# A hybrid attention and SSM layer on one core: SSM before the q/k projection's leftovers, GLU ahead of attention, cache work last, SSM products in pairs

## The chip, the cores and the metric

The kernel runs on one core of a Trainium2 chip. The metric is the device time of one execution in microseconds (us), lower is better. Of the kernel before there are three timed runs, and beside them one profiled execution, from which all rows below come.

## What is computed

One layer, for a prompt of 2048 tokens and a sample of 64 tokens whose past of 1024 keys and values comes from a cache. `proj = x @ w_in` gives q, k, v (512 columns each) and u (512 columns). Half of the width is differential attention (8 heads, two softmax maps each, block-causal), the other half an S5 state space model (SSM) in 32 groups of 16 channels with a 64-dimensional complex state each:

```python
bu = einsum('blgc,gpc->blgp', u, bb)              # input to the states
h  = associative_scan(complex h = lb*h + bu)      # prompt from 0, sample from h0
y  = Re(einsum('blgp,gcp->blgc', h, c)) + d*u     # out of the states
z  = gelu(y) @ w_glu + b_glu ; ssm_out = z[:512] * sigmoid(z[512:])
mix = concat(attention, ssm_out) @ w_out
x1 = LN(alpha*x + mix) ; x2 = LN(alpha*x1 + relu(x1 @ w_up)^2 @ w_down)
```

Outputs are x2, the rotated keys, the values and the last SSM states.

## The kernel before, in words

Large products are done in three passes of float32r pieces (`mm3`, L136 to L139: high by high, low by high, high by low), so an operand is first split into a high part (L131 or L133) and a low part (L134). The SSM's own products are float32 and appear twice per product among the matmul records.

Stages, in the order of the code: `proj_uv` makes u (PSUM tile `pu`) and v (`pv`) for all tokens; `proj_qk` makes q and k (PSUM tile `pm`, transposes `pt`) in 17 tiles of 128 tokens and stores them transposed to DRAM (`s_q`, `s_k`); `attention_all` runs the heads in four sets of query tiles (scores `sps`, transposed weights `tps`, values `oT`); `glu` turns the stored SSM result into the second half of the mix (PSUM `za`, `zb`); `blocks` runs w_out (`pd`), the norm and the feed-forward part (`pu`, `pd`) for four blocks of 512 tokens.

The SSM runs in four batches of eight groups. `ssm_build` makes a batch's matrices: `em` (input), `gf` (powers of the transition), `km` (the direct part, made from the products `psk` and a trip through DRAM, `s_kp`) and `et` (rotations, on POOL). `ssm_run` loads u as `ug`, makes `psi` = em by ug, rotates (`turn`), scans along time (L883), rotates back into `vt`, and then for each group makes `psy` = km by ug plus two products gf by vt (real and imaginary part, 64 rows each: group 2q uses rows 0 to 63, group 2q+1 rows 64 to 127). GELU is made from two ACT and two DVE instructions on `gy`, which is stored to `s_gy`. The GLU loads all of it back (`gyg`, four loads of 1060 KB) with its weights (`wrg`).

`cache_keys` copies the cached values (`cvr` to `s_vc`) and splits the cached keys (`ckr`, `ckh`, `ckl` to `s_kc`). Its result is first read by the sample units of the third attention set.

What sets the order: a scheduler sorts each engine's instructions at build time by readiness and priority. Code under `level(n)` has priority n*100000 above the rest, attention runs at HIP = 200000. While `proj_qk` runs, each of its steps is followed by ten steps of the SSM generator `fl` (priority U8); from step CK0 = 6 on, also by one step of `cache_keys`. The GLU runs as filler of the attention stage at priority U4. Each engine then takes its list strictly in order; all loads and stores go through SP's list, so one that waits holds all behind it.

Of the kernel before, what the change touches and what calls it, by code (L numbers as in the profile page):

```python
# [29 lines left out]
HD = 64  # L30
NMAP = 16
G = 32
PS = 64
C = 16
T = 8
JP = SEQ // T
NJ = JP + 1 + DEC // T
# [29 lines left out]
CK0 = 6  # L67
# [4 lines left out]
U8 = 0  # L72
# [8 lines left out]
U1, U2, U4 = 2, 3, 0  # L81
# [33 lines left out]
def build(nc, tc, io, ctx):  # L115
# [25 lines left out]
    def tt(e, out, a, b, op):  # L141
        e.tensor_tensor(out=out, in0=a, in1=b, op=op)  # L142
# [125 lines left out]
    def split_v(vv, v):  # L268
        split(vv[:, :, 0], vv[:, :, 1], v.rearrange("p (h d) -> p h d", d=HD), hi_eng=dve, lo_eng=pool)
# [125 lines left out]
    def cache_keys(c2):  # L395
        op = c2.enter_context(tc.tile_pool(name="ck", bufs=CKB, side="right"))
        for i in range(PAST // 128):
            raw = op.tile([128, 512], F32, tag="ckr", name="cvr")
            dma(out=raw, in_=io["cv"][i * 128:i * 128 + 128, :])
            for q, t_ in enumerate("hl"):  # L400
                vv = op.tile([128, 4, 2, HD], F32R, tag="ck" + t_, name="cvv")
                split_v(vv, raw[:, q * 256:q * 256 + 256])
                dma(out=VC.rearrange("h p i e d -> p i h (e d)")[:, i, q * 4:q * 4 + 4], in_=vv.rearrange("p h e d -> p h (e d)"))
            if i % 2:
                yield
        for c in range(4):
            for hf in range(2):
                h = op.tile([128, 512], F32R, tag="ckh", name="ckh")
                l = op.tile([128, 512], F32R, tag="ckl", name="ckl")
                rr, cc = slice(c * 128, (c + 1) * 128), slice(hf * 512, hf * 512 + 512)  # L410
                raw = op.tile([128, 512], F32, tag="ckr", name="ckr")
# [5 lines left out]
                yield  # L417
# [264 lines left out]
    def ssm_disc(kp, sp):  # L682
# [62 lines left out]
        ss.dsb = kp.tile([C, G], F32, name="dsb")  # L745
# [11 lines left out]
    def ssm_build(w, bt):  # L757

        ss = k.ss
# [8 lines left out]
        m.gf = w.kp.tile([128, 2, HP, 9, C], F32, tag="gf", name="gf", bufs=MB)  # L770
        m.et = w.kp.tile([128, 2, HP, NJ], F32, tag="et", name="et", bufs=EB)
# [36 lines left out]
        k0 = bp.tile([128, HG, 128], F32, tag="btm", name="k0")[0:C]  # L808
        dd = bp.tile([C, HG, C], F32, tag="dd", name="dd")
        for e in range(2):  # L810
            psk = pm.tile([C, HP, 128], F32, tag="pi", name="psk", bufs=IB)
            o = slice(e * 64, e * 64 + 64)
            for q in range(HP):
                for ri in range(2):
                    pe.matmul(psk[:, q, :], lhsT=bb[o, ri, q, :], rhs=m.gf[o, ri, q, 0:8, :].rearrange("p t c -> p (t c)"),
                              start=ri == 0, stop=ri == 1)
            act.activation(out=k0.rearrange("c (q e) n -> c e q n", e=2)[:, e], in_=psk, func=AF.Copy)
        tt(dve, dd, ss.dsb[:, gs].unsqueeze(2).to_broadcast([C, HG, C]), ident[0:C, 0:C].unsqueeze(1).to_broadcast([C, HG, C]), ALU.mult)
        tt(dve, k0[:, :, 0:C], k0[:, :, 0:C], dd, ALU.add)
        dma(out=KP[:, gs, 112:240], in_=k0)  # L820
# [15 lines left out]
        pool.tensor_copy(out=e[:, :, :, JP:NJ], in_=e[:, :, :, 0:NJ - JP])  # L836
        w.mats = m
        yield

    def ssm_run(w, m, bt):  # L840
# [10 lines left out]
        z = bp.tile([128, 2, HP, NJ], F32, tag="z", name="z", bufs=ZB)  # L851
# [28 lines left out]
        for ri in range(2):  # L880
            for q in range(HP):
                for c0, c1, i in ((0, JP, 0.0), (JP + 1, NJ, h0[:, ri, q:q + 1])):
                    dve.tensor_tensor_scan(out=z[:, ri, q, c0:c1], data0=ss.rho[:, bt * HP + q:bt * HP + q + 1].to_broadcast([128, c1 - c0]),  # L883
                                           data1=v[:, ri, q, c0:c1], initial=i, op0=ALU.mult, op1=ALU.add)
# [4 lines left out]
        for g in range(HG):  # L889
            psy = pm.tile([128, 512], F32, tag="ps", name="psy")  # L890
            y = psy[:, :NJ]
            o = slice(g % 2 * 64, g % 2 * 64 + 64)
            pe.matmul(y, lhsT=m.km[:, g, :], rhs=ug[:, g, :], start=True, stop=False)
# [3 lines left out]
            gy = sp.tile([128, NJ], F32, tag="gy", name="gy", bufs=GB)  # L897
            act.activation(out=gy, in_=y, func=AF.Square, scale=math.sqrt(0.044715))
            dve.scalar_tensor_tensor(out=gy, in0=gy, scalar=1.0, in1=y, op0=ALU.add, op1=ALU.mult)
            act.activation(out=gy, in_=gy, func=AF.Tanh, scale=GC)  # L900
            dve.scalar_tensor_tensor(out=gy, in0=gy, scalar=1.0, in1=y, op0=ALU.add, op1=ALU.mult)
            gg = bt * HG + g
            dma(out=GY[gg * C:(gg + 1) * C, :, :].rearrange("c t j -> t c j"), in_=gy)
            if g % 4 == 3:
                yield
# [326 lines left out]
    with ExitStack() as c1:  # L1232
# [253 lines left out]
```

## Time and profile before

| | us |
|---|---|
| median of three runs | 3104.84 (3096.53 to 3106.6) |
| profiled execution | 3110.11 |
| its span | 3108.3 |
| PE busy | 2884.2 (93%) |
| DVE, ACT, POOL busy | 1755.3, 1504.1, 1649.0 |

The span has these stages: u and v up to about 205 us, q/k with the SSM up to about 525 us, attention set 0 with the GLU up to about 757 us, then w_out and the feed-forward part beside the other attention sets up to about 2030 us, and the feed-forward part of the last blocks alone to the end. A matmul's end is modelled, so the place of a product is best read from where the next one starts.

### The profile page before, as it was taken

The page shows a single profiled execution, that of the slowest core. Times are in us where ns is not written, and L with a number is a line of the kernel's source. Part 1 is how long each engine was busy: PE and PEld are TensorE (multiplying, and loading weights), DVE is VectorE, ACT ScalarE, POOL GpSimd, SP SyncE. Part 2 cuts the span into 40 slices and gives each one's busy share as a digit, 9 for nine tenths or more (in the row PEclk, how much of TensorE's full clock was granted, in tenths as well). Part 3 has the DMA queues.
Part 4 walks back from the last instruction along what each step waited for, and adds up shares of the span by engine and source line. Part 5 has one row for each costly group of instructions (what it writes and reads, how often), then busy time and mean ns, then how long its engine had stood idle before and what let it go on. Part 6 is the DMA issues. An engine that isn't in the chain of part 4 may idle for free.

```text
span 3108.3 us, 46420 instructions
## 1 busy us (share of the span) xinstructions
PE 2884.2 (93%) x15648; PEld 2418.0 (78%) x15648; DVE 1755.3 (56%) x4631; ACT 1504.1 (48%) x2905; POOL 1649.0 (53%) x1552
## 2 busy tenths in 40 slices
PE   8999999799889999999869999988799999989996
PEld 7976666698778888887659888866688888868885
DVE  7126876588687655657787666545526222442224
ACT  4222233687676766665568767532323333323332
POOL 2227762355665566655646656544545444555554
PEclk9999999699989999999879999999899999999998
DMA  6368784656744444445634333266322222253332
GB/s 189 121 200 222 203 231 140 209 160 200 210 133 135 129 127 124 120 128 185 182 107 126 109 106 95 80 196 193 92 84 69 79 82 81 83 169 95 99 99 71
DMA packets 419619, 424.42 MB, mean 137 GB/s; under 512 B 53394, under 2 KB 312978, under 8 KB 418356
## 3 DMA queue, kind: packets, MB, share of 16 engines
q1 hardware_dynamic: 419380, 421.46, 46.6%
q8 instruction: 123, 2.02, 0.3%
q14 instruction: 116, 0.95, 0.1%
HBM read 327.71 MB, written 93.64 MB: 136 GB/s over the span
## 4 chain that ended last, share of the span: by engine, by line
PE 58%; DVE 13%; DMA 10%; issue 4%; ACT 3%; POOL 3%; SPq 1%; DVEq 0%; POOLq 0%; ACTq 0%
PE pd L137 7%; PE pd L138 7%; PE pd L139 7%; PE pu L137 7%; PE pu L139 6%; PE pu L138 6%; PE oT L579 3%; PE tps L563 3%; PE sps L516 2%; DVE acc L142 2%; DMA raw<-in_w_up 2%; DMA raw<-in_ln_g 2%; DVE s L519 2%; ACT s L527 1%; DMA raw<-in_w_out 1%
## 5 line engine op out<-in xcount | busy, mean ns | idle before, releaser
L134 POOL TENSOR_TENSOR dl<-raw,dh 128x512 fp32r<-128x512 f32 x336 | 437.1, 1313 | 312.5 <-ACT dh L131 269.6
L134 POOL TENSOR_TENSOR fwl<-raw,fwh 128x512 fp32r<-128x512 f32 x256 | 332.3, 1301 | 351.6 <-ACT fwh L131 314.1
L519 DVE TENSOR_SCALAR_CACHE_REDUCE s<-sps 128x512 f32<-128x512 f32 (+5 forms) x688 | 401.4, 599 | 192.6 <-PE sps L516 115.6
L137 PE MATMUL pu<-bxh,fwh 128*128 128x256 f32 (+2 forms) x1472 | 490.4, 335 | 14.3 <-ACT fr L1178 8.6
L142 POOL TENSOR_TENSOR s<-s 128x512 f32<-128x512 f32 (+3 forms) x344 | 383.2, 1138 | 206.8 <-ACT s L547 182.8
L138 PE MATMUL pu<-bxl,fwh 128*128 128x256 f32 (+2 forms) x1472 | 487.0, 332 | 0.0
L139 PE MATMUL pu<-bxh,fwl 128*128 128x256 f32 (+2 forms) x1472 | 483.7, 333 | 1.9 <-POOL fwl L134 1.7
L137 PE MATMUL pd<-dh,hh 128*128 128x512 f32 (+1 forms) x1088 | 427.1, 398 | 13.3 <-DVE hh L133 6.3
L138 PE MATMUL pd<-dl,hh 128*128 128x512 f32 (+1 forms) x1088 | 429.0, 395 | 0.3 <-POOL dl L134 0.3
L139 PE MATMUL pd<-dh,hl 128*128 128x512 f32 (+1 forms) x1088 | 417.0, 395 | 3.3 <-POOL hl L134 1.9
L527 ACT ACTIVATE s<-s,nm 128x1024 f32<-128x1024 f32 (+9 forms) x416 | 365.6, 881 | 109.2 <-DVE nm L524 105.7
L142 DVE TENSOR_TENSOR acc<-acc,pd 128x512 f32<-128x512 f32 (+1 forms) x384 | 253.8, 682 | 261.7 <-PE pd L139 258.9
L131 ACT ACTIVATE dh<-raw 128x512 fp32r<-128x512 f32 x336 | 209.2, 628 | 375.2 <-PE pd L139 157.7
L133 DVE CAST hh<-fr 128x256 fp32r<-128x256 f32 (+2 forms) x184 | 114.6, 623 | 389.6 <-ACT fr L1179 379.8
L137 PEld LDWEIGHTS pu<-bxh,fwh 128*128 128x128 f32 x1472 | 280.8, 191 | 46.8 <-ACT fr L1178 12.3
L131 ACT ACTIVATE fwh<-raw 128x512 fp32r<-128x512 f32 x256 | 160.6, 628 | 316.7 <-DMA raw<-in_w_up 166.9
L139 PEld LDWEIGHTS pu<-bxh,fwl 128*128 128x128 f32 x1472 | 278.7, 191 | 29.2 <-POOL fwl L134 3.8
L138 PEld LDWEIGHTS pu<-bxl,fwh 128*128 128x128 f32 x1472 | 280.8, 191 | 26.1
L579 PE MATMUL oT<-w,vt 128*128 128x256 f32 (+3 forms) x1296 | 256.0, 297 | 14.6 <-ACT w L131 6.4
L137 PEld LDWEIGHTS pd<-dh,hh 128*128 128x128 f32 (+1 forms) x1088 | 201.5, 186 | 58.8 <-DVE hh L133 9.2
L516 PE MATMUL sps<-kst,qst 96*128 96x512 f32 (+2 forms) x544 | 218.7, 422 | 30.5 <-DVE s L519 28.2
L579 PEld LDWEIGHTS oT<-w,vt 128*128 128x128 f32 (+1 forms) x1296 | 207.4, 197 | 43.3 <-DVE w L134 12.4
(273 smaller groups left out, 5905.6 us busy)
## 6 DMA issues: line engine op xcount, KB each, us to landing
raw<-in_w_up SPq DMA_DIRECT2D x256, 256.0 KB
raw<-in_w_down SPq DMA_DIRECT2D x256, 256.0 KB
kst<-s_k SPq DMA_DIRECT2D x64, 384.0 KB
raw<-in_w_out SPq DMA_DIRECT2D x80, 256.0 KB
xr<-in_xT SPq DMA_DIRECT2D x64, 256.0 KB
vt<-s_v SPq DMA_DIRECT2D x32, 512.0 KB
qst<-s_q SPq DMA_DIRECT2D x64, 192.0 KB
s_q<-tph SPq DMA_DIRECT2D x34, 256.0 KB
```

The source lines that it names most:

```text
L131: act.activation(out=dst_hi, in_=src, func=AF.Copy)
L133: hi_eng.tensor_copy(out=dst_hi, in_=src)
L134: (lo_eng or dve).tensor_tensor(out=dst_lo, in0=src, in1=dst_hi.bitcast(F32), op=ALU.subtract)
L137: pe.matmul(ps, lhsT=lh, rhs=rh, start=start, stop=False)
L138: pe.matmul(ps, lhsT=lh, rhs=rl, start=False, stop=False)
L139: pe.matmul(ps, lhsT=ll, rhs=rh, start=False, stop=stop)
L142: e.tensor_tensor(out=out, in0=a, in1=b, op=op)
L516: pe.matmul(ps[:nr, :e - c0], lhsT=qst[m][0:96, q], rhs=self.keys(m, 96, c0, e), start=True, stop=True)
L519: dve.tensor_scalar(out=s[:nr, o:o + c1 - c0], in0=ps[:nr, :c1 - c0], scalar1=1.0, scalar2=None, op0=ALU.mult, op1=ALU.max, accum_out=self ...
L527: act.activation(out=x, in_=x, func=AF.Exp, bias=nm, accum_out=self.ls[:nr, m, p:p + 1])
L563: pe.transpose(out=ps[:kr, i * nr:i * nr + nr], in_=self.s[t, 0, k_ * 128 // SC][:nr, o:o + kr], identity=ident[:nr, :nr])
L579: pe.matmul(self.oT[:, t * nr:(t + n) * nr], lhsT=vt[k_ // 8][:kr, k_ % 8, :], rhs=w[:kr, e, i * nr:(i + n) * nr], start=(k_ == 0 and e == ...
```

## The change

- The SSM steps beside `proj_qk` get priority 1 (U8), the GLU priority 3, above attention (U4).
- The cache work starts one step early, keeps the lowest priority and is no longer spread by CK0; its pieces are half or a quarter as wide.
- `psk` is made for two groups in one product from a zero-padded copy `bz` of `bb`.
- One scan of 1064 columns per real or imaginary part takes the place of eight: a tile `rh` of factors, zero where prompt and sample begin, resets it. ACT copies both parts of `psi`.
- In the last loop two groups are worked on in turn: both km products, then the gf products alternating between the two.

```diff
-CK0 = 6
-U8 = 0
+U8 = 1
-U1, U2, U4 = 2, 3, 0
+U1, U2, U4 = 2, 3, 3
...
         for i in range(PAST // 128):
-            raw = op.tile([128, 512], F32, tag="ckr", name="cvr")
...
-            if i % 2:
-                yield
+            for q in range(4):
+                raw = op.tile([128, 256], F32, tag="ckr", name="cvr")[:, 0:128]
+                dma(out=raw, in_=io["cv"][i * 128:i * 128 + 128, q * 128:q * 128 + 128])
+                vv = op.tile([128, 2, 2, HD], F32R, tag="ck" + "hl"[q % 2], name="cvv")
+                split_v(vv, raw)
+                dma(out=VC.rearrange("h p i e d -> p i h (e d)")[:, i, q * 2:q * 2 + 2], in_=vv.rearrange("p h e d -> p h (e d)"))
+            yield
         for c in range(4):
-            for hf in range(2):
+            for hf in range(4):
+                h = op.tile([128, 256], F32R, tag="ckh", name="ckh")
...
         for e in range(2):
-            psk = pm.tile([C, HP, 128], F32, tag="pi", name="psk", bufs=IB)
             o = slice(e * 64, e * 64 + 64)
-            for q in range(HP):
-                for ri in range(2):
-                    pe.matmul(psk[:, q, :], lhsT=bb[o, ri, q, :], rhs=m.gf[o, ri, q, 0:8, :].rearrange("p t c -> p (t c)"),
+            pool.tensor_copy(out=bz[o, :, :, e, :], in_=bb[o])
+        psk = pm.tile([2 * C, HP, 128], F32, tag="pi", name="psk", bufs=IB)
+        for q in range(HP):
+            for ri in range(2):
+                pe.matmul(psk[:, q, :], lhsT=bz[:, ri, q].rearrange("p e c -> p (e c)"), rhs=m.gf[:, ri, q, 0:8, :].rearrange("p t c -> p (t c)"),
...
+        pool.tensor_copy(out=m.rh, in_=ss.rho[:, qs].unsqueeze(2).to_broadcast([128, HP, NJ + 1]))
+        pool.memset(m.rh[:, :, 0:JP + 2:JP + 1], 0.0)
...
-                if ri == 0:
-                    act.activation(out=z[:, ri, q, :], in_=psi[:, :NJ], func=AF.Copy)
-                else:
-                    dve.tensor_copy(out=z[:, ri, q, :], in_=psi[:, :NJ])
+                act.activation(out=z[:, ri, q, :], in_=psi[:, :NJ], func=AF.Copy)
...
         for ri in range(2):
-            for q in range(HP):
-                for c0, c1, i in ((0, JP, 0.0), (JP + 1, NJ, h0[:, ri, q:q + 1])):
-                    dve.tensor_tensor_scan(out=z[:, ri, q, c0:c1], data0=ss.rho[:, bt * HP + q:bt * HP + q + 1].to_broadcast([128, c1 - c0]),
+            dve.tensor_tensor_scan(out=zt[:, ri].rearrange("p q j -> p (q j)"), data0=m.rh.rearrange("p q j -> p (q j)"),
...
-        for g in range(HG):
+        for q in range(HP):
+            ys = [pm.tile([128, 512], F32, tag="ps", name="psy")[:, :NJ] for e in range(2)]
+            for e, y in enumerate(ys):
+                pe.matmul(y, lhsT=m.km[:, 2 * q + e, :], rhs=ug[:, 2 * q + e, :], start=True, stop=False)
             for ri in range(2):
-                pe.matmul(y, lhsT=m.gf[o, ri, g // 2, 1:9, :].rearrange("p t c -> p (t c)"), rhs=vt[o, ri, g // 2, 0:NJ], start=False, stop=ri == 1)
+                for e, y in enumerate(ys):
+                    o = slice(e * 64, e * 64 + 64)
+                    pe.matmul(y, lhsT=m.gf[o, ri, q, 1:9, :].rearrange("p t c -> p (t c)"), rhs=vt[o, ri, q, 0:NJ], start=False, stop=ri == 1)
...
             ck = cache_keys(c2)
+            next(ck)
             for i, _ in enumerate(urgent(proj_qk(wq, wk, xp, x0, c2), U6)):
...
-                if i >= CK0:
-                    next(ck, None)
             run(ck)
```

On PE, in the third SSM batch, the products of a pair of groups (`psy`, numbered; `km` and `gf` are their matrices) stand like this before:

```order
L893 MATMUL psy_3375<-ug_3049,km_2796 128x265
L895 MATMUL psy_3375<-vt_3059,gf_2798 128x265 x2
L893 MATMUL psy_3385<-ug_3049,km_2796 128x265
L895 MATMUL psy_3385<-vt_3059,gf_2798 128x265 x2
```

and now:

```order
L897 MATMUL psy_3374<-ug_3044,km_2807 128x265
L897 MATMUL psy_3375<-ug_3044,km_2807 128x265
L901 MATMUL psy_3374<-vt_3054,gf_2809 128x265
L901 MATMUL psy_3375<-vt_3054,gf_2809 128x265
L901 MATMUL psy_3374<-vt_3054,gf_2809 128x265
L901 MATMUL psy_3375<-vt_3054,gf_2809 128x265
```

The two groups now alternate; but the scheduler sorts these products too, and not every pair stands so.

On PE, where the q/k projection ends and attention begins, the last rows of the SSM stand like this before (`sps` are attention's scores):

```order
L893 MATMUL psy<-ug,km 128x265
L895 MATMUL psy<-vt,gf 128x265 x2
L518 MATMUL sps<-kst,qst 128x128
L516 MATMUL sps<-kst,qst 128x256
...
L518 MATMUL sps<-kst,qst 128x128
L893 MATMUL psy<-ug,km 128x265
L895 MATMUL psy<-vt,gf 128x265 x2
L893 MATMUL psy<-ug,km 128x265
L895 MATMUL psy<-vt,gf 128x265 x2
L563 MATMUL tps<-ident,s 128x128 x7
L893 MATMUL psy<-ug,km 128x265
L895 MATMUL psy<-vt,gf 128x265 x2
```

and now:

```order
L349 MATMUL pt<-ident,qk 128x128 x8
L897 MATMUL psy<-ug,km 128x265 x2
L901 MATMUL psy<-vt,gf 128x265 x4
L349 MATMUL pt<-ident,qk 128x128 x6
L517 MATMUL sps<-kst,qst 128x128
L515 MATMUL sps<-kst,qst 128x256
L517 MATMUL sps<-kst,qst 128x128
L349 MATMUL pt<-ident,qk 128x128 x2
L897 MATMUL psy<-ug,km 128x265
L901 MATMUL psy<-vt,gf 128x265 x2
L897 MATMUL psy<-ug,km 128x265
L901 MATMUL psy<-vt,gf 128x265 x2
```

Six groups come after the last projection product before, three of them behind 30 scores; now four groups do, the last two behind three scores.

On SP, around the last load of the SSM's result for the GLU (`gyg`), before:

```order
L126 DMA s_gy<-gy 8x16x265
L126 DMA bg<-in_bglu 128x8
L126 DMA s_o<-o 128x2x64
L126 DMA vt<-s_v 128x512
L126 DMA wrg<-in_w_glu 128x1024 x2
```

and now, from the last stores of the SSM's result (`s_gy`) on:

```order
L125 DMA s_gy<-gy 8x16x265 x2
L125 DMA s_kc<-tph 128x4x64 x2
L125 DMA s_kc<-tpl 128x4x64
L125 DMA s_kc<-ckh 128x256 x2
L125 DMA s_kc<-ckl 128x256
L125 DMA ckr<-in_ckT 128x256
L125 DMA gyg<-s_gy 128x2120
L125 DMA qst<-s_q 96x512
```

A piece of the cached keys (three stores that wait for POOL, one load) now stands ahead of that load and of the next head's queries; seven such pieces stand in SP's list between the start of attention and the GLU's first results.

## Rows read from the trace of the kernel before

**Rows 1.** The page: busy us, share of the span, instructions.
```profile
PE 2884.2 (93%) x15648; PEld 2418.0 (78%) x15648; DVE 1755.3 (56%) x4631; ACT 1504.1 (48%) x2905; POOL 1649.0 (53%) x1552
```
**Rows 2.** Busy time by stretch: start:end, length, busy us (records) by engine, clock, DMA share.
```profile
core 0: us, PE busy (x) PEld busy (x) DVE busy (x) ACT busy (x) POOL busy (x), PEclk, DMA share, GB/s
205.00:530.00 325.00, 300.53 (x1418) 214.74 (x1416) 226.15 (x349) 91.78 (x190) 192.46 (x297) 0.97 0.77 206
530.00:610.00 80.00, 58.11 (x236) 45.67 (x237) 47.22 (x202) 51.89 (x147) 23.00 (x29) 0.57 0.73 217
610.00:760.00 150.00, 144.74 (x1159) 140.16 (x1158) 126.14 (x456) 118.16 (x278) 83.75 (x101) 0.99 0.54 158
760.00:900.00 140.00, 117.54 (x588) 95.36 (x588) 106.94 (x331) 101.12 (x182) 96.72 (x83) 0.89 0.68 205
```
**Rows 3.** Instruction groups from 205 to 530 us: busy us, mean ns.
```profile
L815 PE MATMUL psk<-gf,bb 64*16 64x128 f32 x128 | 15.8, 306 | 6.9 <-ACT em L805 4.9 <-POOL gf L142 1.8 <-DVE gf L796 0.2
L883 DVE TENSOR_TENSOR_SCAN z<-rho,vt 128x256 f32<-128x256 f32 x32 | 22.7, 709 | 0.0
L883 DVE TENSOR_TENSOR_SCAN z<-rho,h,vt 128x8 f32<-128x8 f32 x32 | 6.9, 216 | 0.0
L867 DVE COPY z<-psi 128x265 f32<-128x265 f32 x16 | 6.8, 426 | 8.2 <-PE psi L863 8.2
```
**Rows 4.** PE in order of time: start us, length us; two places in the SSM.
```profile
319.03 0.72 PE L895 MATMUL psy<-vt,gf 64*128 64x265 f32 x4 [1.29 <-DVE vt L142]
319.68 0.50 PE L138 MATMUL pm<-wl,xh 128*128 128x512 f32 x1
...
333.55 0.71 PE L893 MATMUL psy<-ug,km 128*128 128x265 f32 x2
334.19 1.16 PE L895 MATMUL psy<-vt,gf 64*128 64x265 f32 x4
335.28 0.71 PE L893 MATMUL psy<-ug,km 128*128 128x265 f32 x2
```
**Rows 5.** Chain of work, 520 to 610 us: start us, length us.
```profile
525.65 4.31 DMA kst<-s_k
...
536.98 5.61 DMA kst<-s_k
542.65 2.34 DMA qst<-s_q
...
547.27 3.20 DMA s_gy<-gy
...
553.91 4.63 DMA s_k<-tpl
...
567.26 11.61 DMA qst<-s_qm
```
**Rows 6.** The tile gy: DVE's last step, first and last start.
```profile
L901 DVE SCALAR_TENSOR_TENSOR gy<-gy,psy x32: 418/426/433, 331.7 to 567.5; 128x265 f32<-128x265 f32 x32
```
**Rows 7.** PE where the projection ends.
```profile
523.54 0.39 PE L139 MATMUL pm<-wh,xl 128*128 128x512 f32 x1
```
**Rows 8.** The tile gyg: its loads on SP.
```profile
L126 SPq DMA_DIRECT2D gyg<-s_gy x4: 343/423/424, 564.2 to 583.4; - x4
```
**Rows 9.** SP's waits, 205 to 530 us: us in total, times, longest.
```profile
SPq L126 <- POOL ckh L133: 17.7, 6, 4.9
```
**Rows 10.** SP in order of time: one cheap issue after another.
```profile
585.69 0.31 SPq L126 DMA_DIRECT2D kst<-s_k  x1
```
**Rows 11.** The tile zb: the GLU's products, first and last start.
```profile
L137 PE MATMUL zb<-gh,whg x128: 276/281/562, 589.3 to 751.7; 128*128 128x256 f32 x112, 128*128 128x320 f32 x16
```

More of the change, by code (lines that the diff above doesn't have):

```diff
@@ L397, in cache_keys @@
         for i in range(PAST // 128):
-            raw = op.tile([128, 512], F32, tag="ckr", name="cvr")
[L399 to L403, printed above, removed]
-            if i % 2:
-                yield
-        for c in range(4):
-            for hf in range(2):
[L408 to L411, printed above, removed]
+            for q in range(4):
[5 more added lines that the diff above has]
+            yield
+        for c in range(4):
+            for hf in range(4):
+                h = op.tile([128, 256], F32R, tag="ckh", name="ckh")
+                l = op.tile([128, 256], F32R, tag="ckl", name="ckl")
+                rr, cc = slice(c * 128, (c + 1) * 128), slice(hf * 256, hf * 256 + 256)
+                raw = op.tile([128, 256], F32, tag="ckr", name="ckr")
                 dma(out=raw, in_=io["ckT"][rr, cc])
@@ L744, in ssm_disc @@
         dma(out=KP[:, :, 0:112], in_=ss.zz.to_broadcast([C, G, 112]))
-        ss.dsb = kp.tile([C, G], F32, name="dsb")
+        ss.dsb = kp.tile([2 * C, G // 2], F32, name="dsb")
+        ss.id2 = kp.tile([2 * C, C], F32, name="id2")
+        tt(dve, ss.id2, ident[0:2 * C, 0:C], ident[0:2 * C, C:2 * C], ALU.add)
         dma(out=ss.dsb, in_=io["dT"])
@@ L770, in ssm_build @@
         m.gf = w.kp.tile([128, 2, HP, 9, C], F32, tag="gf", name="gf", bufs=MB)
+        m.rh = w.kp.tile([128, HP, NJ + 1], F32, tag="rh", name="rh", bufs=EB)
         m.et = w.kp.tile([128, 2, HP, NJ], F32, tag="et", name="et", bufs=EB)
@@ L807, in ssm_build @@
         yield
-        k0 = bp.tile([128, HG, 128], F32, tag="btm", name="k0")[0:C]
-        dd = bp.tile([C, HG, C], F32, tag="dd", name="dd")
+        k0 = bp.tile([128, HG, 128], F32, tag="btm", name="k0")[0:2 * C, 0:HP]
+        dd = bp.tile([2 * C, HP, C], F32, tag="dd", name="dd")
+        bz = bp.tile([128, 2, HP, 2, C], F32, tag="bz", name="bz")
+        pool.memset(bz, 0.0)
         for e in range(2):
-            psk = pm.tile([C, HP, 128], F32, tag="pi", name="psk", bufs=IB)
             o = slice(e * 64, e * 64 + 64)
-            for q in range(HP):
-                for ri in range(2):
-                    pe.matmul(psk[:, q, :], lhsT=bb[o, ri, q, :], rhs=m.gf[o, ri, q, 0:8, :].rearrange("p t c -> p (t c)"),
-                              start=ri == 0, stop=ri == 1)
-            act.activation(out=k0.rearrange("c (q e) n -> c e q n", e=2)[:, e], in_=psk, func=AF.Copy)
-        tt(dve, dd, ss.dsb[:, gs].unsqueeze(2).to_broadcast([C, HG, C]), ident[0:C, 0:C].unsqueeze(1).to_broadcast([C, HG, C]), ALU.mult)
+            pool.tensor_copy(out=bz[o, :, :, e, :], in_=bb[o])
[3 more added lines that the diff above has]
+                pe.matmul(psk[:, q, :], lhsT=bz[:, ri, q].rearrange("p e c -> p (e c)"), rhs=m.gf[:, ri, q, 0:8, :].rearrange("p t c -> p (t c)"),
+                          start=ri == 0, stop=ri == 1)
+        act.activation(out=k0, in_=psk, func=AF.Copy)
+        tt(dve, dd, ss.dsb[:, qs].unsqueeze(2).to_broadcast([2 * C, HP, C]), ss.id2.unsqueeze(1).to_broadcast([2 * C, HP, C]), ALU.mult)
         tt(dve, k0[:, :, 0:C], k0[:, :, 0:C], dd, ALU.add)
-        dma(out=KP[:, gs, 112:240], in_=k0)
+        for e in range(2):
+            dma(out=KP.rearrange("c (q e) n -> e c q n", e=2)[e, :, qs, 112:240], in_=k0[e * C:e * C + C])
         for n in range(T):
@@ L849, in ssm_run @@
             dma(out=ug[(7 - s) * C:(8 - s) * C, :, :], in_=US.rearrange("(g c) s j -> s c g j", c=C)[s, :, gs, :])
-        z = bp.tile([128, 2, HP, NJ], F32, tag="z", name="z", bufs=ZB)
+        zt = bp.tile([128, 2, HP, NJ + 1], F32, tag="z", name="z", bufs=ZB)
+        z = zt[:, :, :, 1:NJ + 1]
         vt = bp.tile([128, 2, HP, NJ + 1], F32, tag="vt", name="vt")
@@ L888, in ssm_run @@
         yield
-        for g in range(HG):
[L890 to L893, printed above, removed]
-            for ri in range(2):
-                pe.matmul(y, lhsT=m.gf[o, ri, g // 2, 1:9, :].rearrange("p t c -> p (t c)"), rhs=vt[o, ri, g // 2, 0:NJ], start=False, stop=ri == 1)
[L897 to L904, printed above, removed]
+        for q in range(HP):
+            ys = [pm.tile([128, 512], F32, tag="ps", name="psy")[:, :NJ] for e in range(2)]
+            for e, y in enumerate(ys):
+                pe.matmul(y, lhsT=m.km[:, 2 * q + e, :], rhs=ug[:, 2 * q + e, :], start=True, stop=False)
+            for ri in range(2):
+                for e, y in enumerate(ys):
+                    o = slice(e * 64, e * 64 + 64)
+                    pe.matmul(y, lhsT=m.gf[o, ri, q, 1:9, :].rearrange("p t c -> p (t c)"), rhs=vt[o, ri, q, 0:NJ], start=False, stop=ri == 1)
+            gs_ = [sp.tile([128, NJ], F32, tag="gy", name="gy", bufs=GB) for e in range(2)]
+            for y, gy in zip(ys, gs_):
+                act.activation(out=gy, in_=y, func=AF.Square, scale=math.sqrt(0.044715))
+                dve.scalar_tensor_tensor(out=gy, in0=gy, scalar=1.0, in1=y, op0=ALU.add, op1=ALU.mult)
+            for e, (y, gy) in enumerate(zip(ys, gs_)):
+                act.activation(out=gy, in_=gy, func=AF.Tanh, scale=GC)
+                dve.scalar_tensor_tensor(out=gy, in0=gy, scalar=1.0, in1=y, op0=ALU.add, op1=ALU.mult)
+                gg = bt * HG + 2 * q + e
+                dma(out=GY[gg * C:(gg + 1) * C, :, :].rearrange("c t j -> t c j"), in_=gy)
+            if q % 2:
                 yield
@@ L1462 @@
         bP=bP, cP=cP,
[L1463 removed]
+        dT=f["ssm_d"][0].reshape(16, 2, C).transpose(1, 2, 0).reshape(2 * C, 16), h0=np.stack([pair(f["state_ssm_re"][0, 0]), pair(f["state_ssm_im"][0, 0])], 1),
         w_glu=f["w_glu"][0], bglu=f["b_glu"][0].reshape(8, 128).T, w_out=f["w_out"][0],
```

6 lines of the change are left out of this document (3 added, 3 removed).

## The prediction

> **What bounds the kernel now.** I read the page's busy times first: PE is busy for 2884 us of the span, 93%, every other engine for 57% or less [rows 1]. So PE is the bound wherever it is fed, and the question for each part of the change is whether PE had too much to do or too little there. The busy time by stretch answers that [rows 2]. From 205 to 530 us (q/k projection with the SSM) PE is busy for 300.5 of 325 us at a clock of 0.97 of 2.4 GHz: work bounds it, with 24.5 us of waits. From 530 to 610 us it is busy for 58.1 of 80 us at 0.57, so most of this stretch runs at the 1.2 GHz level. From 610 to 760 us (GLU and attention) it is full again: 1159 products in 150 us, 0.129 us each. At that pace the 236 products of the 80 us would take 30.5 us; some 49.5 us are lost where attention begins. That is the largest hole that the change comes near to.
>
> The chain of waits says what that hole is made of [rows 5]: loads of keys and queries, a store of the SSM's result, a store of transposed keys, and then 11.6 us for a query load of a few KB. SP issued three GLU loads of 1060 KB each just before, from 564.2 us on [rows 8]; the small load, issued 3 us later, lands when they are through. The filler that could keep PE busy, the GLU, waits for the SSM's last result: its last step on DVE begins at 567.5 us [rows 6], 44 us after the last projection product at 523.54 us [rows 7].
>
> **The change part by part, first the SSM's work on PE (all from 205 to 530 us, on the bound engine).** The products psk take 15.8 us in 128 records [rows 3]. There are 64 products now and 32 after, over all 128 rows in place of 64, with the same 128 columns streamed. No row shows the new form. If its price is that of the old form, half goes, 7.9 us; if the doubled rows double it, nothing does. I take 7.9, since the row gives 0.123 us a record and no sign that rows count.
>
> The gf products in turn: at 319.03 us two of them that belong to two groups happen to stand side by side in the kernel before, and the next product starts 0.65 us later. At 334.19 us two of the same group stand side by side, and the next starts 1.09 us later [rows 4]. Both begin after something other and end before something other, so the difference, 0.44 us, is what running in different rows at once gives per pair. If all 32 possible pairs were new this would be 14 us. The order of PE's list says otherwise: 8 such pairs stand there already, 19 after the change, because the scheduler pulls some apart again. Eleven new pairs give 4.8 us.
>
> Passing from a product over all rows to one over half of them also costs: the km product at 333.55 us holds PE for 0.64 us until the gf products start, though its two records need 0.22 us each where the same kind follows (two gf products of one group, 1.09 us with four records and one such passage, give the same: 0.87 + 0.22) [rows 4]. So a passage is about 0.2 us. I count 134 passages around psi, psk and psy in PE's list before and 111 after: 23 fewer, 4.6 us. The Trainium skill (TensorEngine Tiling (Array Packing), Key Properties) says that changing the tiling mode, not just the tile, drains TensorE; by that rule alone a pair that the scheduler splits into km, gf, km, gf would gain nothing and the sum of this paragraph and the one before would be 4.6 us in place of 9.4.
>
> Together 17.3 us of PE time. I take all of it, since PE is 92% busy here; it is 0 if the chain of the SSM sets the stage, and 17.3 + 24.5 = 41.8 if the waits go with it.
>
> **SSM work on the other engines.** The scans take 22.7 + 6.9 = 29.6 us [rows 3]. Between 8 and 256 columns the time grows by (709 - 216) / 248 = 2.0 ns a column, over a base of 200 ns. Eight scans of 1064 columns then take 8 x 2.33 = 18.6 us: DVE is freed of 11 us. The 16 copies of z, 6.8 us, pass from DVE to ACT, which is busy for 92 of 325 us. POOL gets copies (bz, rh) of a size that no row shows alone; by the 2.0 ns a column of DVE's scan above and nothing below, 1064 columns of rh and four small ones are 0 to 3 us a batch, beside 192 of 325 us busy. I cost all of this at nothing: PE's projection products hide it. It makes each batch's chain shorter by about 4 us, which shows in the next term. If that cover is gone, POOL's copies cost up to 12 us.
>
> **Where attention begins.** Before, six groups of the SSM come after the last projection product and take 44 us to finish, 7.3 us each; after, four do, and the last two stand behind three scores in place of 30. At the same price the GLU's last input is ready 2 x 7.3 = 15 us sooner. Against it stand seven pieces of cached keys in SP's list, three stores and a load each. In the q/k stage such a store held SP for 17.7 / 6 = 2.95 us when it waited for POOL [rows 9], and an issue takes 0.31 us [rows 10]. All waiting, that is 7 x (2.95 + 4 x 0.31) = 29 us; none waiting, 8.7 us, in a list that had gaps. The queries of the next heads and the GLU's last load are queued behind them, and PE waits for those. POOL is busy for only 23 of 80 us there, and the pieces are half as wide, so I take 12 us, nearer to the lower end. This term is -3 us. Its bounds are -49.5 (the hole goes altogether) and +29.
>
> **GLU ahead of attention.** No product is added or removed. At the first feed-forward product PE's list has 68 fewer attention products behind it than before; they come later, into the start of w_out, where PE is idle for 140 - 117.5 = 22.5 us and the clock is at 0.89 [rows 2]. At 0.129 us each they are 8.8 us. Attention also waits for ACT and DVE, so I count about half, -5 us; bounds -8.8 and, if the attention they belong to ends later by as much, +8.8.
>
> **Cache work in the q/k stage.** 76 more DMAs go through SP's list over the whole change, nearly all here: 24 us of issuing at 0.31 us, spread over 325 us, beside projection products whose inputs are loaded a block ahead. I take 0; if each new wait for POOL holds SP and then PE, the price is that of the slower rival below.
>
> **Sum.** -17.3 - 3 - 5 = -25.3 us. The profiled execution took 3110.1 us (span 3108.3 and 1.8 around it), which gives 3084.8. It lies 5.3 us above the median of the runs, 3104.8, so I forecast 3080.
>
> **Rivals.**
> A. The hole where attention begins closes. For it: the GLU has the highest priority and its input is ready sooner. Against it: the three large loads still stand ahead of the second heads' queries in SP's list, so those 11.6 us stay, and the first scores still wait for loads issued after the last projection product. 45 of 49.5 us would go: 3104.8 - 17 - 5 - 45 = 3038. Chance 0.12.
> B. The SSM's saving is hidden. The stage would be set by the batches' chain through POOL, DVE and DRAM, and by loads (DMA share 0.77), so that PE merely idles more. For it: 24.5 us of waits are there now. Against it: only a few of these are at psy, and PE is at full clock. About -3 us: 3102. Chance 0.15.
> C. Slower: SP is held by the cache pieces. Place: SP's list from the first query loads to the GLU's weights. All seven pieces wait, 29 us, and the same happens once to a projection block's input; the SSM's 17 us come off. 3104.8 + 30 - 17 = 3118. It decides from the point where the pieces hold SP for more than 37 us over the whole of it, or for 20 us with half of the SSM's saving hidden. For it: POOL's list has cached keys between attention's additions, which wait for ACT, and SP's list has the stores between query loads. Against it: POOL is idle most of that time. Chance 0.18.
>
> **How the numbers follow.** The forecast has 0.55; its own range is 3060 to 3098. A difference under 0.3%, 9.3 us, can't be told from none. Faster by more: all of A, and all but 0.03 of the forecast's 0.55, gives 0.64. Within 0.3%: 0.12 of B, 0.03 of the forecast and 0.03 of C, 0.18. Slower: 0.15 of C and 0.03 of B, whose hidden saving would bring POOL's copies into the open: 0.18. The range for 8 in 10 reaches to A's and C's values: 3037 to 3119.
>
> **What would show it.** Right: psk in 64 records and about 8 us; gf products of two groups a few ns apart; PE's share from 205 us to the last projection product higher and that product some 15 us sooner, near 508 us; the first GLU product within 60 us of it (66 us before, at 589.3 [rows 11]); a half-clock stretch of 50 to 70 us. Wrong: the last projection product not sooner than 518 us (B); SP waiting for POOL's ckh between the first scores and the first GLU products for over 15 us (C); no half-clock stretch there (A). A gain or loss that comes after 900 us would be of another cause than any named here.

## The result: slower by 0.6%

| | before | after |
|---|---|---|
| median of 9 runs each, us | 3100.35 (3092.73 to 3113.25) | 3120.48 (3113.94 to 3124.09) |
| ratio, 95% interval | | 1.0058 (1.0046 to 1.0070) |
| profiled span, us | 3108.3 | 3120.6 |
| PE busy / not busy, us | 2884.2 / 224.1 | 2868.8 / 251.8 |

Forecast were 3080 us, a range of 3037 to 3119 and 0.64 for faster. The profiled execution of before lay 10 us above its median, so the spans show 12 us of the 18 to 20. PE's busy time fell by 15.4 us and its idle time rose by 27.7. The 15.4 look like the 17.3 of the sum, but only 11.6 of them are at psk and psy, and busy time also moves with the granted clock: e5 below, which takes no product away, is busy for 2876.2 us, 8 less than before.

Where the idle time rose, the busy time by stretch tells (columns as in [rows 2]). It stands after the busy times of the whole execution:

```profile
PE 2868.8 (92%) x15584; PEld 2408.3 (77%) x15584; DVE 1740.9 (56%) x4576; ACT 1508.2 (48%) x2917; POOL 1671.2 (54%) x1604
```
```profile
205.00:530.00 325.00, 284.16 (x1300) 202.88 (x1299) 213.87 (x287) 89.78 (x198) 212.74 (x336) 0.95 0.73 189
530.00:610.00 80.00, 48.83 (x202) 37.20 (x200) 37.83 (x155) 38.92 (x111) 20.34 (x29) 0.66 0.79 239
610.00:760.00 150.00, 142.05 (x1139) 138.69 (x1140) 113.86 (x417) 110.96 (x274) 77.77 (x100) 0.96 0.57 166
760.00:900.00 140.00, 119.06 (x594) 95.26 (x592) 106.30 (x344) 101.60 (x184) 91.56 (x79) 0.90 0.75 216
```

PE idles 40.8 us in the first stretch (24.5 before) and 31.2 in the second (21.9 before); the later ones are within 3 us. So PE's added idle time lies from 205 to 610 us: 72.0 us in place of 46.4. The tiles' rows after (count: shortest/median/longest ns, first and last start in us) show the order of events:

```profile
L138 PE MATMUL pm<-wh,xl x272: 387/389/795, 215.8 to 540.6; 128*128 128x512 f32 x136
L517 PE MATMUL sps<-kst,qst x256: 222/282/583, 552.6 to 2030.4; 99*128 99x256 f32 x66, 99*128 99x128 f32 x62
L136 PE MATMUL zb<-gh,whg x128: 275/280/522, 606.7 to 749.6; 128*128 128x256 f32 x112, 128*128 128x320 f32 x16
L821 PE MATMUL psk<-gf,bz x64: 272/273/422, 255.2 to 446.0; 128*32 128x128 f32 x64
L888 DVE TENSOR_TENSOR_SCAN z<-rh,vt x8: 2352/2357/2792, 311.1 to 512.7; 128x1064 f32<-128x1064 f32 x8
L844 POOL COPY rh<-rho x4: 1080/3236/4574, 225.9 to 454.3; 128x1064 f32<-128x1064 f32 x4
```

The last projection product comes at 540.6 us, 17 us later than in [rows 7], where the prediction wanted it 15 us sooner. The projection's loads are late too. SP's last load of x (xr), before and then after:

```profile
L126 SPq DMA_DIRECT2D xr<-in_xT x72: 367/388/1608, 2.1 to 486.3; - x72
```
```profile
L125 SPq DMA_DIRECT2D xr<-in_xT x72: 368/390/1239, 2.1 to 503.0; - x72
```

It too is 17 us later. That alone doesn't say which held which, since a load also waits for its buffer, and PE's own waits for pieces of x (xh and xl) are only 6.4 us here (none before); most of the rest of its idle time is spread over the SSM's products. What SP itself waited for longest from 205 to 541 us (total, times, longest) is the cache work: 34.0 us for value pieces, where the kernel before has 9.9 from 205 to 530. For key pieces it waits less, 10.3 us in place of the 17.7 of [rows 9]; together that is 44.3 for 27.6.

```profile
SPq L125 <- POOL cvv L133: 34.0, 14, 5.5
SPq L125 <- POOL ckh L132: 10.3, 6, 3.2
```
```profile
SPq L126 <- POOL cvv L134: 9.9, 7, 6.2
```

The loads of the pieces show what one piece costs. Before:

```profile
L126 SPq DMA_DIRECT2D cvr<-in_cv x8: 352/591/1136, 213.3 to 305.4; - x8
L126 SPq DMA_DIRECT2D ckr<-in_ckT x8: 382/523/1104, 320.0 to 433.9; - x8
```

After:

```profile
L125 SPq DMA_DIRECT2D cvr<-in_cv x32: 357/443/1397, 213.7 to 468.4; - x32
L125 SPq DMA_DIRECT2D ckr<-in_ckT x16: 333/424/866, 473.7 to 626.5; - x16
```

Each piece goes through one load buffer: load, DVE and POOL (a key piece POOL alone), store, next load. A value piece takes (468.4 - 213.7) / 31 = 8.2 us, a key piece (626.5 - 473.7) / 15 = 10.2. The 48 pieces make a chain whose last step on POOL (ckl) starts at 630 us instead of 440, beside the projection and through the start of attention.

### The profile page after: what moved, and what is told of

It is laid out like the page before. It is cut to its first block, busy times and chain, and to the rows that moved or that the text cites. A ratio compares the mean times of both kernels' runs of the same rounds, so it can differ in the third digit from the quotient of the medians.

```text
span 3120.6 us, 46439 instructions
## 1 busy us (share of the span) xinstructions
PE 2868.8 (92%) x15584; PEld 2408.3 (77%) x15584; DVE 1740.9 (56%) x4576; ACT 1508.2 (48%) x2917; POOL 1671.2 (54%) x1604
## 4 chain that ended last, share of the span: by engine, by line
PE 54%; DVE 11%; DMA 11%; POOL 5%; issue 3%; ACT 2%; SPq 2%; DVEq 0%; POOLq 0%; ACTq 0%
PE pd L136 7%; PE pd L137 7%; PE pd L138 7%; PE pu L136 6%; PE pu L138 6%; PE pu L137 6%; PE oT L578 3%; PE tps L562 3%; PE sps L515 3%; DVE acc L141 2%; DMA raw<-in_ln_g 2%; DMA raw<-in_w_up 2%; DVE s L518 2%; SPq L125 2%; DMA raw<-in_w_out 1%
## 5 line engine op out<-in xcount | busy, mean ns | idle before, releaser
L133 POOL TENSOR_TENSOR fwl<-raw,fwh 128x512 fp32r<-128x512 f32 x256 | 332.8, 1303 | 339.0 <-ACT fwh L130 315.2
L132 DVE CAST hh<-fr 128x256 fp32r<-128x256 f32 (+2 forms) x184 | 108.0, 587 | 377.6 <-ACT fr L1187 372.7
```

The source lines that it names most:

```text
L132: hi_eng.tensor_copy(out=dst_hi, in_=src)
L133: (lo_eng or dve).tensor_tensor(out=dst_lo, in0=src, in1=dst_hi.bitcast(F32), op=ALU.subtract)
```

## The experiments

Ratios are to the kernel before on the same chip. "Stage" is from the first to the last projection product, "gap" from there to the first score, "idle" PE's from 205 to 610 us, all from one profiled execution (before: 311.5, 6.7, 46.4; changed kernel: 325.8, 12.0, 72.0).

| run | what | ratio, 95% | stage | gap | idle |
|---|---|---|---|---|---|
| e1 | changed, cache of before | 1.0378 (1.0362 to 1.0393) | 313.9 | 5.7 | 66.3 |
| e2 | before + SSM arithmetic | 1.0279 (1.0264 to 1.0294) | 310.6 | 6.1 | 61.8 |
| e3 | changed, U8 = 0 | 1.0093 (1.0076 to 1.0110) | 316.0 | 14.6 | 67.8 |
| e4 | changed, U4 = 0 | 1.0099 (1.0084 to 1.0114) | 327.7 | 11.1 | 69.4 |
| e5 | before + narrow cache | 1.0063 (1.0049 to 1.0077) | 337.9 | 19.6 | 64.9 |
| e6 | changed, U8 = U4 = 0 | 1.0069 (1.0052 to 1.0087) | 319.7 | 13.1 | 72.5 |
| e7 | changed, POOL stores pieces | 1.0081 (1.0061 to 1.0101) | 315.2 | 12.9 | 62.8 |
| e8 | changed, old scan, no rh | 1.0038 (1.0023 to 1.0052) | 318.9 | 11.4 | 57.0 |
| e9 | e8 + cache of before | 1.0003 (0.9990 to 1.0017) | 301.5 | 5.2 | 45.9 |
| e10 | before + psk + pairs | 0.9984 (0.9971 to 0.9997) | 304.9 | 5.2 | 49.9 |
| e11 | changed, 16 value pieces | 0.9989 (0.9977 to 1.0001) | 315.5 | 11.6 | 61.7 |
| e12 | before + U8, U4 | 1.0067 (1.0047 to 1.0087) | 329.0 | 6.7 | 47.4 |
| e13 | changed, keys copied | 1.0117 (1.0096 to 1.0138) | 319.9 | 6.1 | 58.1 |
| e14 | before + U8 | 1.0066 (1.0046 to 1.0086) | 308.2 | 6.0 | 32.4 |
| e15 | e10 + U4 | 0.9985 (0.9973 to 0.9997) | 305.7 | 5.4 | 48.5 |
| e16 | e11, U8 = U4 = 0 | 1.0059 (1.0040 to 1.0078) | 316.0 | 7.9 | 61.8 |
| e17 | before + psk | 1.0013 (0.9999 to 1.0026) | 302.3 | 4.8 | 43.6 |
| e18 | before + pairs | 0.9985 (0.9971 to 0.9999) | 309.7 | 4.9 | 39.7 |

**Is it the cache work, and why are its pieces narrow? (e1, e2, e5)**

```diff
 # e1: changed kernel with cache_keys and its pacing of before; e2: also U8 = U4 = 0
-            next(ck)
+                if i >= CK0:
+                    next(ck, None)
 # e5: kernel before with the changed cache_keys, next(ck) ahead of the loop, no CK0
```

> The changed kernel with the cache work of the kernel before (512-column pieces, one step after each projection step from CK0 = 6 on). Cache theory: the pieces hold SP (34 us of waits for cvv in this stage of the changed kernel, 9.9 us before) and so the loads of the projection; without them the last projection product comes at 510 to 520 us in place of 540.6 and the time is 3085 to 3100 us. POOL theory: rh and bz (17 us of POOL) hold the SSM, so the last projection product stays at 530 us or later and the time is 3110 or more. Order theory (the SSM's priority holds the projection): also 3110 or more, with the SSM's last products earlier than the projection's.

> The kernel before with the SSM's arithmetic of the changed kernel alone (psk for two groups, one scan with rh, products in pairs); cache, SSM and GLU priorities as before. Cache theory: the arithmetic saves what was forecast or half of it, last projection product at 508 to 518 us (523.5 before), 3085 to 3095 us. POOL theory: rh (3.0 us a batch) and bz stand in the SSM's chain and eat the saving: last projection product at 523 us or later, 3100 to 3110 us.

> The kernel before with the cache work of the changed kernel alone (narrow pieces, one step early, not paced); SSM arithmetic and priorities as before. Cache theory (72 more waits and issues in SP's list, split of narrow pieces at 0.87 us each on POOL): slower than before by 15 to 30 us, 3112 to 3127, last projection product at 530 to 540 us. Arithmetic theory (rh and bz on POOL and the single scan lengthen the SSM's chain): within 8 us of before, last projection product at 520 to 528 us.

e1 and e2 came out far from where any theory had put them, at 3215 and 3183 us. The stage of e1 is 12 us shorter than the changed kernel's, with the last projection product at 526.6 us between the two ranges given; e2's comes at 523.1, no sooner than before. But the loads of the pieces and of the GLU's weights in e1 stand elsewhere:

```profile
L126 SPq DMA_DIRECT2D cvr<-in_cv x8: 363/480/542, 560.6 to 627.3; - x8
L126 SPq DMA_DIRECT2D wrg<-in_w_glu x4: 333/352/425, 719.4 to 731.1; - x4
```

The cache work starts only when the SSM is over (last psy at 529.3 us), and the GLU's weights only when the last key piece is through (ckl, 716.0 us); the GLU's first product falls from 607 to 727 us. With rh gone (e9) the same wide pieces start at 215.5 us again, and narrow ones beside rh start at 213.7 us (changed kernel); only wide pieces beside rh start late. So the narrow pieces are what rh's memory costs. And they are dear: e5, which has the changed cache work (narrow pieces, early start, no spreading) and nothing else, is 20 us slower than before, as much as the whole change, with a stage of 338 us. Here SP waits 41.5 us for cvv from 205 to 610 us:

```profile
SPq L126 <- POOL cvv L134: 41.5, 15, 7.2
SPq L126 <- POOL ckh L133: 21.3, 9, 3.9
```

Yet PE hardly idles more up to 530 us (columns as in [rows 2]):

```profile
205.00:530.00 325.00, 295.92 (x1343) 208.71 (x1341) 209.60 (x354) 86.39 (x182) 184.91 (x306) 0.93 0.70 179
```

It is idle for 29.1 us (24.5 before), but at a granted clock of 0.93 in place of 0.97, and 768 of the projection's 816 records are through in place of all. So the late end of this stage isn't idle time alone. The lower clock has a share in this trace, but it is seen in a faster run too (0.94 in e10), so how much of the pieces' price it is stays open.

**SP, the number of pieces, or their end? (e7, e11, e13)**

```diff
 # e7: the stores of the pieces
-        sync.dma_start(...)
+        pool.dma_start(...)
 # e11: values; ckh is now 512 columns wide
-            for q in range(4):   # 128 columns, buffers ckh and ckl in turn
+            for q in range(2):   # 256 columns, buffer ckh
 # e13: keys, 12 transfers, no split
-                split(h, l, raw, hi_eng=pool, lo_eng=pool)
+                    dma(out=KC[rr, j, 0:PAST], in_=io["ckT"][rr, :])
```

> The changed kernel with the cache pieces' stores issued by POOL, which makes the pieces, instead of SP; loads stay on SP. SP then never waits for cvv and ckh (34.0 and 15.8 us between 205 and 600 us in the changed kernel). Cache theory by SP: last projection product 10 to 17 us sooner (524 to 531) and 3095 to 3108 us. If it is POOL's or the DMA's time that the pieces cost and not SP's, no gain: 3115 to 3130, since POOL now issues 64 stores as well.

> The changed kernel with its cached values in 16 pieces of 256 columns in place of 32 of 128 (one buffer for the split values, of double width); cached keys as narrow as in it. Cache theory by the number of pieces: the values are half of the added work (36 of the 72 added DMAs and 12 of the added us of POOL), so 6 to 12 us are back, 3105 to 3113, last projection product 5 to 12 us sooner. If single buffering is what counts (one piece at a time, now also for the split values): no gain, 3115 to 3128.

> The changed kernel with its 32 narrow value pieces, but the cached keys copied unsplit by 12 transfers from DRAM to DRAM (the split of the cached keys into high and low parts is left out). Tail theory: what costs is that the chain of pieces, 8 to 10 us each whatever the width, does not end before the last projection product, so that key pieces stand among attention's first loads; without them the first scores come within 8 us of the last projection product (12 us in the changed kernel) and the time is 3090 to 3102. Count theory: each narrow piece beside the projection costs, and all 32 are still there: last projection product at 533 to 545 us and 3108 to 3120.

e11 takes 16 of 48 pieces away and wins back all: 3096 us, by the ratios 21 us less than the changed kernel, more than expected. Its loads and SP's waits from 205 to 610 us:

```profile
L125 SPq DMA_DIRECT2D cvr<-in_cv x16: 352/500/1608, 210.8 to 362.9; - x16
L125 SPq DMA_DIRECT2D ckr<-in_ckT x16: 374/435/713, 373.0 to 519.8; - x16
```
```profile
SPq L125 <- POOL ckh L132: 16.0, 8, 4.4
SPq L125 <- POOL cvv L133: 12.0, 4, 5.2
```

A piece of twice the width takes (362.9 - 210.8) / 15 = 10.1 us, against 8.2: most of the price is one per piece. The chain's last step on POOL starts at 523 us and the last projection product comes at 527.3. But the stage, at 315.5 us, and the idle time, at 61.7, stay above those before, so the gain isn't read from them alone; and the same 16 pieces taken away with both priorities as before (e16 against e6) bring 0.1%, within the noise, though SP waits for pieces no longer there (25.4 us for cvv and ckh) than before (27.6). A price per piece, or SP's wait, does not by itself set the time.

e7 moves the last projection product to 526.2 us, as the SP theory said, and its profiled execution took 3113 us, but the median of its six is 3128, so there is no gain. It isn't the clean test that was meant either: SP was to wait for cvv no more, but it still does, and for the landing of loads besides (205 to 610 us):

```profile
SPq L125 <- POOL cvv L133: 21.0, 13, 4.2
SPq L125 <- DMA cvr<-in_cv: 17.9, 9, 3.3
```

POOL now issues the stores (busy us, mean ns), and the SSM's last product psy comes at 576.6 us, 16 us later than in the changed kernel:

```profile
L125 POOL DMA_DIRECT2D s_vc<-cvv x32 | 23.9, 748 | 2.5 <-POOL cvv L133 2.5
L125 POOL DMA_DIRECT2D s_kc<-ckh x22 | 12.2, 554 | 0.3 <-POOL ckh L132 0.3
```

e13's transfers run at the start and put the first projection product at 228.4 us, 14 us late, so its total can't be compared. Its stage can: without any key piece it is still 320 us; only the gap shrinks, from 12.0 to 6.1. So the key pieces make 6 us of the stage and 6 us of the gap; what is left of the longer stage, 8 us over before, is there with the value pieces alone.

**The arithmetic (e6, e8, e9, e10, e17, e18)**

```diff
 # e8: the scan of before, m.rh and its two POOL instructions removed
-            dve.tensor_tensor_scan(out=zt[:, ri]..., data0=m.rh..., initial=0.0)
+            for q in range(HP):
+                for c0, c1, i in ((0, JP, 0.0), (JP + 1, NJ, h0[:, ri, q:q + 1])):
...
 # e9: e8 and the cache work of before; e10: e9 with U8 = U4 = 0
 # e17: before, psk from bz alone; e18: before, products of two groups in turn alone
```

> The changed kernel with both priorities as before (U8 = 0 and U4 = 0): arithmetic and cache work alone. Each alone gave 8 to 11 us over the changed kernel; if they add, 3135 to 3145 here. With the run of the new cache alone it tells what the arithmetic is worth beside narrow pieces: cache theory, this one is 10 to 17 us faster than the new cache alone; arithmetic theory, 15 us or more slower.

> The changed kernel with the 64 short scans of before and without rh. DVE gets back about 10 us, POOL loses 12 us of rh copies, which stand in the chain of waits for 3 to 4.6 us a batch. Arithmetic theory: last projection product 8 us sooner or more, 3105 to 3112. Cache theory: within 5 us of the changed kernel.

> The changed kernel with the short scans of before and no rh, and with the room that rh leaves free used for the cache pieces of before (512 columns, CK0 = 6): psk for two groups, products in pairs and both priorities remain. Cache theory (the narrow pieces alone cost the 20 us): last projection product at 505 to 518 us and 3075 to 3092 us, faster than both kernels. If the arithmetic's saving is hidden in any case: 3093 to 3103, last projection product at 518 to 526.

> The kernel before with psk for two groups and the products in pairs alone; scans, cache pieces and priorities as before. Forecast: these take 17.3 us off PE's work, so 3080 to 3090 us. If the chain hides it: 3095 to 3103 with PE's busy time down by 10 us or more and its idle time up by as much.

> The kernel before with psk for two groups alone (bz on POOL, 64 products' records in place of 128); products of one group at a time, z copies, scans, cache and priorities as before. The term as forecast, 7.9 us of PE off the bound engine: 3087 to 3093 if before runs at 3098. If it is half (psk took 10.0 us in place of 15.8 beside the narrow pieces) and partly hidden: 3093 to 3099.

> The kernel before with the products of two groups in turn alone. The term as forecast, 9.4 us of PE: 3085 to 3092 if before runs at 3098. Rival: both PSUM tiles of a pair come free together and late, so PE waits for gy in place of vt (12.6 us of such waits in the run with psk and pairs, 5.3 before), and the gain is gone: 3095 to 3101, with the products psy shorter by 4 us or more and the waits for gy longer by as much.

e6 against e5: with narrow pieces the arithmetic shortens the stage by 18 us and the time by nothing. e8 gains some 6 us on the changed kernel (the intervals overlap), in the range of its first expectation, with the last projection product 7 us sooner: there is no sign that the one scan with rh pays. e9 has the shortest stage of all and equals before, no better. e10 (which also has both copies of psi on ACT) gains 0.16%, 5.0 us, under a third of its forecast. From e10 to the changed kernel there are three steps: both priorities, 0.9984 to 1.0003 (e9); the changed cache work, to 1.0038 (e8); the one scan with rh, to 1.0058. That is 6, 11 and 6 us, and of these only the 11 of the cache work are clear of the noise. e17 and e18 share e10's gain out: psk gains nothing, the pairs 0.15%. The pairs do what was said; PE in e18 in order of time (start, length; the next start is the measure):

```profile
331.92 1.16 PE L892 MATMUL psy<-ug,km 128*128 128x265 f32 x4
333.01 1.16 PE L896 MATMUL psy<-vt,gf 64*128 64x265 f32 x8
334.10 1.11 PE L863 MATMUL psi<-ug,em 128*64 128x265 f32 x6
```

Two groups take 2.18 us; in [rows 4] one takes 1.73, two 3.46. All psy products together are busy for 49.1 us (57.2 before), 8.1 less, for 9.4 forecast; PE's waits for gy are 5.9 us (5.3 before), so the rival of e18 is out.

**The priorities (e3, e4, e12, e14, e15, e16)**

```diff
 # e12: before;  e14: the first line alone;  e15: e10 with the second line alone
-U8 = 0
+U8 = 1
-U1, U2, U4 = 2, 3, 0
+U1, U2, U4 = 2, 3, 3
 # e3, e4: changed kernel with the first, the second taken back;  e16: e11 with both
```

> The changed kernel with the SSM at its old priority beside the projection (U8 = 0). Order theory: the last projection product returns to 525 us or sooner and the time falls by 10 us or more, to 3110 or less. Cache theory and POOL theory: SP and POOL are held as before, 3115 to 3125 us, and the last projection product stays within 8 us of 540.

> The changed kernel with the GLU at its old priority, behind attention (U4 = 0). If the GLU ahead of attention is worth the 5 us forecast, this is slower than the changed kernel by 3 to 9 us (3123 to 3130). If what it wins until the GLU's end (14 us in the changed kernel's trace) is given back by the attention left over, it is within 3 us of the changed kernel. If it costs, 3110 or less. The last projection product does not move (540 us).

> The kernel before with the two priorities alone (U8 = 1, U4 = 3). Forecast for the GLU ahead of attention, -5 us, and nothing of size for the SSM first: 3090 to 3098. If what the GLU wins is given back later: 3098 to 3104. If the SSM's priority holds the projection (last projection product 532.5 in the run with both priorities as before, 540.6 in the changed kernel): last projection product at 528 to 535 us and 3103 to 3112.

> The kernel before with the SSM's priority alone (U8 = 1). The two priorities together cost 20 us on the kernel before, with the last projection product 16 us later. If it is the SSM's priority: last projection product at 533 to 543 us and 3108 to 3120 us. If it is the GLU's: last projection product at 520 to 527 and 3092 to 3101.

> The kernel before with psk for two groups, the products in pairs, and the GLU ahead of attention (U4 = 3): the run with psk and pairs alone, 0.9984 of before, and one priority more. If the GLU ahead is worth the 5 us forecast: 3083 to 3091, the best so far. If what it wins up to the GLU's end is given back: within 4 us of the run without it, 3090 to 3098.

> The changed kernel with value pieces of 256 columns and both priorities as before: arithmetic with the one scan, and 32 pieces in place of 48. If the SSM's priority holds the projection here too: last projection product sooner than 520 us and 3078 to 3090. If the priorities do nothing beside narrow pieces: within 5 us of the run with them, 3091 to 3101.

On the kernel before, the SSM's priority costs 0.66%, by itself (e14) as with the GLU's (e12); e14's eleven times lie between 3102 and 3132 us, and the profiled one is the 3102, so its stage of 308 us doesn't show the loss, while e12's of 329 does. The GLU's priority is worth nothing where nothing else disturbs (e15 against e10). With narrow pieces the signs turn: taking either back costs 0.35 to 0.4% (e3, e4), both 0.1% (e6), and both in e11 0.7% (e16, where neither expectation had it). The effects don't add, and these runs don't say why.

## Why the prediction was wrong, step by step

- **Cache work beside the projection, costed at 0: the step that failed.** I counted SP's issues (24 us, spread) and weighed only the waits for ckh. Its price alone is 0.63%, 20 us (e5), and 0.35%, 11 us, beside the rest of the change without the one scan (e9 to e8). What goes with it in the traces: the pieces wait by turns for load, DVE and POOL in one buffer, SP stands at the stores for 44.3 us in place of 27.6, and the projection's loads and its last product come 17 us later. That SP's waits are the way by which the time is lost is argued and not shown: e7 took away only part of them and gained nothing, and e5 shows a lower clock besides. Nor does a run part the width of the pieces from their early start without spreading.
- **Rival C** (3118, chance 0.18) named SP held by the pieces and nearly the time, but the wrong place, so that the time agrees by luck. It looked at seven key pieces from the first query loads on and wanted over 15 us of waits for ckh between the first score and the first GLU product; there SP has none. The value pieces' waits are in the 300 us before, and the key pieces' share of the gap was 6 us. Its second break-even is a slip as well: 37 less the 17.3 is 20 us with the whole of the saving hidden; with half of it hidden it is 28.
- **SSM work, -17.3 us.** In the changed kernel psk fell from 15.8 to 10.0 us of busy time and psy from 57.2 to 51.4, 11.6 together, a third less than the term. The time gained is less still: on the kernel before, psk brings 0 and the pairs 4.6 us (0.3 to 9.0). I took work off a bound engine at its full price. In e10, which gains 5.0 us, psk and psy together fall only by 5.5 (to 12.2 and 55.3), PE idles 3.5 us more from 205 to 610 us, and the stage is 6.6 us shorter. So rival B, that the saving turns into idle time, holds for a part; and the clock was lower, granted at 0.94 from 205 to 530 us in place of 0.97. The median psk of e10 takes 421 ns, that of the changed kernel 273:

```profile
L821 PE MATMUL psk<-gf,bz x64: 272/421/422, 246.8 to 437.1; 128*32 128x128 f32 x64
```

- **SSM ahead of the projection (U8), no term at all.** The sum has nothing for it and gives no reason. On the kernel before it costs 0.66% (e14); in the changed kernel taking it back costs 0.35% more (e3). The loss stands with both priorities as before (e6, 1.0069), so it doesn't need this one.
- **Broken pairs.** The Trainium skill (TensorEngine Tiling (Array Packing), Key Properties) says that changing the tiling mode drains TensorE, from which I took it that a pair split into km, gf, km, gf gains nothing. In the changed kernel such a run from 335.87 to 339.33 us takes 3.46 us, twice the 1.73 of one group before [rows 4]; the trace agrees that nothing is gained.

```profile
335.87 0.71 PE L897 MATMUL psy<-ug,km 128*128 128x265 f32 x2
336.51 1.16 PE L901 MATMUL psy<-vt,gf 64*128 64x265 f32 x4
337.60 0.71 PE L897 MATMUL psy<-ug,km 128*128 128x265 f32 x2
338.25 1.16 PE L901 MATMUL psy<-vt,gf 64*128 64x265 f32 x4
339.33 0.50 PE L137 MATMUL pm<-wl,xh 128*128 128x512 f32 x1
```

- **Scan and copies, costed at 0.** A scan's median is 2.36 us for 2.33 forecast. rh takes 3.0 us in the mean, the upper end given for all of POOL's new copies of a batch. Scan and rh together cost some 6 us (e8, not clear of the noise) in place of 0, and rh's memory forces the narrow pieces: that cost was in room, which I didn't look at.
- **Attention's start, -3 us.** The last psy came 3 us sooner (560.4) after a projection that ended 17 us later, for 15 forecast; the first GLU product comes 66 us after the last projection product, as before, and PE idles 9 us more from 530 to 610.
- **GLU ahead of attention, -5 us.** From the GLU's first product to its last, 757.8 us, the stage is 14 us shorter (151.1 for 165.3). The last transposes of the mix (nps) come at 2103 us in place of 2052, but that isn't shown to be the price: with this priority alone added they come sooner (2040 us in e15, 2048 in e10). Its worth is 0 beside the wide pieces (e15 against e10) and 0.4%, 13 us, in the changed kernel (e4).

## What to carry to other kernels

Price a piece of side work by its round trip through its buffer (8.2 us for 128 columns, 10.1 for 256), and look at what its stores may hold up in an in-order queue; halving the pieces doubles the trips. Look at what memory a change takes and which other work has to shrink for it. The work forecast to leave the busiest engine is an upper bound on the gain: here 5 of 17 us arrived (1 to 9 by the interval). And test a change's parts in company as well as alone: the same priority cost 20 us in one kernel and saved 11 in another.

## What the runs showed of the hardware

The gf products of two groups in different rows run wholly at once: eight records in 1.09 us, the time of four of one group. And the same POOL instruction can vary sixfold: the subtraction that makes a value piece of 256 columns takes 722 to 775 ns in e1, where it runs after the SSM, and 722 to 4369 beside it in the kernel before. The Trainium skill (SBUF — State Buffer, Who interferes with whom) says that VectorE and GpSimd share a pair of ports, and that, where a VectorE instruction with two SBUF inputs meets a GpSimd one that reads SBUF, the second to issue waits for the other's whole instruction. In length these rows fit that: the long one starts at 313.49 us, and DVE's products vt and vx, with two inputs each, then take 2.35 and 1.24 us, together the 3.6 us that are over. In order they don't, since POOL's record starts 0.25 us before that of vt, and no run takes DVE's work away beside POOL's, so the cause is not shown. The rows of e1 and of the kernel before, and the place (start, length):

```profile
L134 POOL TENSOR_TENSOR cvv<-cvr,cvv x16: 722/726/775, 568.2 to 633.7; 128x256 fp32r<-128x256 f32 x16
```
```profile
L134 POOL TENSOR_TENSOR cvv<-cvr,cvv x16: 722/737/4369, 219.0 to 317.8; 128x256 fp32r<-128x256 f32 x16
```
```profile
313.49 6.07 POOL L134 TENSOR_TENSOR cvv<-cvr,cvv 128x256 fp32r<-128x256 f32 x2 [9.65 <-DVE cvv L133]
313.74 2.35 DVE L142 TENSOR_TENSOR vt<-z,et 128x2120 f32<-128x2120 f32 x1
316.02 1.24 DVE L142 TENSOR_TENSOR vx<-z,et 128x1060 f32<-128x1060 f32 x1
```
